# A hybrid encoder block on one core: the attention product in steps of 512 queries, six tiles of P, one tile of diagonals, and low parts of weights on VectorE

## The chip, the core and the metric

The kernel runs on one core of a Trainium2 chip. The core has five engines with an instruction queue each: TensorE (PE in the profile; its weight loads are listed apart as PEld), VectorE (DVE), ScalarE (ACT), GpSimd (POOL) and SyncE (SP), which here issues the DMA transfers. An engine runs its queue in order and waits where an operand or a buffer isn't ready. The metric is the device time of one execution in microseconds, the median of several runs.

## What is computed

One layer of an encoder block over 512 tokens of width 1024: attention heads and state-space heads beside each other, then a gated feed-forward part with a short convolution.

```python
h = rmsnorm(x, norm1_w)
q, k, v, z, xbc, dt_f, dt_b = split(h @ w_in)      # 1024 -> 6176
attn = dilated_attention(partial_rope(q), partial_rope(k), v)     # 16 heads of 64
ssm  = ssm_mixer(z, xbc, dt_f, dt_b, ...)          # 16 heads, 4 groups, chunks of 128, both directions
x = x + concat([attn, ssm]) @ w_out                # 2048 -> 1024
h = rmsnorm(x, norm2_w)
x = x + (silu(gate) * up) @ w_down                 # u = conv(h @ w_up), 1024 -> 2 x 2816 -> 1024
return rmsnorm(x, final_norm_w)
```

The three dilated windows of the attention are computed as one softmax over all 512 keys: each score gets the logarithm of the number of windows in which the pair occurs, or a large negative number where it is in none. All is in float32. Each matrix operand is held as a high and a low part, and a product is the sum of three products (high with high, high with low, low with high), so a matrix product costs three matmuls.

## The kernel before

**Tiles and stages.** Activations lie as 128 partitions by 512 tokens. Weights come by DMA into `raw` tiles; `unit` (L462) splits each into two halves of 128 by 512, a high part `whi` (a copy on ScalarE) and a low part `wlo` (the difference of the two), six buffers each. Which engine makes a difference is read from the table `ENG` (L34), where "A" is ScalarE, "D" VectorE and "P" GpSimd, and a string of several letters is gone through in turn: "lc" and "lx" (the state-space inputs C and X), "lk" (the keys' projections) and "lo" (the output projection) name the low parts that the change touches.

After the first norm comes the woven part. `weave` (L988) takes 50 jobs: eight query and eight key projections (q0 to q7, k0 to k7), three value and three gate projections (the first of each stands ahead of the weave), for each of four groups the inputs B, C and X, the chunk states (s) and the outputs (o) of the state-space part, and eight attention pairs (a0 to a7, two heads each). Each job is a Python generator; its `yield`s divide it into pieces, and `PLAN` (L23) gives each job a due time for its start and its end. At every turn the piece with the earliest due time whose buffers are free goes next. What a `yield` gives back is the piece's share of the job's time; a dictionary names buffers that the next piece needs. This gives a first order of all instructions.

**The order on the engines.** `list_schedule` (L179) then simulates the program with the durations of `cost` (L88), engine by engine, takes the best of some forward and backward passes, and the program is built again with that order fixed on each engine's queue. In the pass (`forward`, L249) an instruction marked as using the port that VectorE and GpSimd share is made longer when the other of the two is busy with such an instruction: by 1 - 0.38 of the other's rest for VectorE, by 1 - 0.8 for GpSimd, with an upper limit (L276 to 280).

**Attention** (`attention_pair`, L926). For each head and each half of the queries (two tiles of 128): two score tiles, each of two matmuls over 512 keys into the bank `s`; VectorE adds the logarithms and takes the minimum (P), ScalarE exponentiates. Then, for two key tiles at a time, four transposes of 128 by 128 into the bank `tr`; ScalarE copies the bank to the high part `PT`, VectorE subtracts it from the bank into the low part `PT`; and four matmuls over 256 queries multiply by the values `V` into the bank `o`. `P` and `PT` have four buffers each, and `tr`, `s` and `o` one bank each.

**Other parts that are named below.** `rope_rows` (L880) ends a projection of q or k: ScalarE copies the bank, VectorE shuffles it (which frees the bank; projections alternate between two banks named `acc`), VectorE multiplies one copy, GpSimd the other, and GpSimd adds them; then follow a high part and a low part, and in `prep_k` (L910) six copies by DMA that spread K over the halves of its tiles. `conv_silu` (L694) evacuates the banks of B, C and X. In `ssm_out` (L796) each of 16 chunks has a tile of decays `D`, two buffers (pool "work", L352): eight diagonals from ScalarE, a scan and two steps on VectorE, and matmuls into the bank `y`. The output projection `out_part` (L1057) starts while the last attention pairs run; the feed-forward part (`up_job`, L1147, and the loop behind it) is one unbroken stream of matmuls.

## Time and profile before

| | |
|---|---|
| median of three runs | 898.53 us (898.29 to 898.71) |
| the profiled execution | 898.54 us |
| its span in the trace | 896.7 us |
| mean granted clock of TensorE | 0.997 of full speed |
| TensorE busy | 881.9 us, 98% |
| VectorE busy | 617.0 us, 69% |
| ScalarE busy | 463.5 us, 52% |
| GpSimd busy | 220.4 us, 25% |
| DMA | 40% of 16 engines, 117 GB/s |

The span runs from the first to the last instruction in the trace; what the execution has beyond it lies around the span. The busy time of an engine is the time in which it has an instruction, waits for a port included. All engine instructions go through one helper, so they all bear line 142, and are told apart by the names of their tiles: `acc<-H,whi` is a matmul into a bank acc with the operands H and whi. A matmul's own duration in a row is longer than the distance to the next, because matmuls are pipelined; the distance between starts is what one costs.

### The profile page before, as it was taken

What the parts mean: (1) busy time and instruction counts of PE and PEld (TensorE: products, weight loads), DVE (VectorE), ACT (ScalarE), POOL (GpSimd) and SP (SyncE); (2) the same over time, 40 slices, a digit from 0 to 9 for tenths busy, and PEclk for the clock granted to TensorE, in tenths of its full rate; (3) what the DMA queues carried; (4) which work ended last, traced back from release to release, by engine and by line L of the source; (5) the groups of instructions that cost most, each with busy time, mean ns of one, the idle gap of its engine ahead of it and who ended that gap; (6) DMA issues with size and microseconds to landing.
All of it is one profiled execution on the core that took longest, in us unless ns stands there. A gap on an engine that the chain in (4) does not pass through costs nothing.

```text
span 896.7 us, 13139 instructions
## 1 busy us (share of the span) xinstructions
PE 881.9 (98%) x4892; PEld 764.9 (85%) x4892; DVE 617.0 (69%) x1038; ACT 463.5 (52%) x963; POOL 220.4 (25%) x187
## 2 busy tenths in 40 slices
PE   7999999999999999999999999999999999999997
PEld 6977888998899889899988998888888888888886
DVE  6766788877896897899843347777777777523323
ACT  6444666556666765767854344444444444323222
POOL 1072564234262543275255300000000000000000
PEclk9999999999999999999999999999999999999999
DMA  8465154534444634235475223333333333222312
GB/s 272 130 146 148 45 124 136 154 85 128 111 113 107 148 111 130 69 92 176 140 240 183 90 77 95 107 103 94 95 94 94 95 111 114 104 95 71 118 48 94
DMA packets 121936, 105.04 MB, mean 117 GB/s; under 512 B 5776, under 2 KB 97808, under 8 KB 121872
## 3 DMA queue, kind: packets, MB, share of 16 engines
q1 hardware_dynamic: 121872, 104.20, 40.1%
q8 instruction: 38, 0.62, 0.3%
q14 instruction: 26, 0.21, 0.1%
HBM read 88.91 MB, written 5.83 MB: 106 GB/s over the span
## 4 chain that ended last, share of the span: by engine, by line
PE 53%; DMA 1%; DVE 0%; ACT 0%; issue 0%; POOLq 0%; POOL 0%; SPq 0%; DVEq 0%; ACTq 0%
PE acc L142 20%; PE tr L142 11%; PE s L142 10%; PE o L142 4%; PE E L142 3%; PE y L142 3%; PE trp L142 2%; DMA mx<-mixA_d 1%; DMA mixA_d<-m 0%; DVE m L142 0%; DVE x L142 0%; ACT fk L142 0%; ACT hl L142 0%; ACT wkp L142 0%; POOLq L1284 0%
## 5 line engine op out<-in xcount | busy, mean ns | idle before, releaser
L142 ACT ACTIVATE whi<-raw 128x512 fp32r<-128x512 f32 x256 | 159.9, 630 | 228.6 <-PE acc L142 142.6
L142 DVE TENSOR_TENSOR wlo<-raw,whi 128x512 fp32r<-128x512 f32 x196 | 140.3, 719 | 135.3 <-ACT whi L142 133.3
L142 PE MATMUL acc<-H,whi 128*128 128x512 f32 x512 | 169.5, 404 | 2.4 <-DVE wkp L142 2.4
L142 POOL TENSOR_TENSOR wlo<-raw,whi 128x512 fp32r<-128x512 f32 x60 | 91.5, 1531 | 131.2 <-ACT whi L142 126.1
L142 PEld LDWEIGHTS acc<-H,whi 128*128 128x128 f32 x512 | 94.1, 190 | 19.9 <-DVE wkp L142 2.8
L142 PE MATMUL acc<-x2w,whi 128*128 128x512 f32 x352 | 109.1, 390 | 0.0
L142 PE MATMUL acc<-H,wlo 128*128 128x512 f32 x256 | 103.1, 403 | 0.0
L142 POOL TENSOR_TENSOR r<-m,half 128x1 f32<-128x1 f32 x4 | 2.2, 548 | 359.2 <-DVE m L142 359.2
L142 PE MATMUL acc<-whi,H 128*128 128x256 f32 x448 | 87.3, 287 | 0.9 <-DVE H L142 0.7
L142 PEld LDWEIGHTS acc<-x2w,whi 128*128 128x128 f32 x352 | 66.0, 188 | 13.7
L142 DVE SCALAR_TENSOR_TENSOR fk<-fk,prm,fk 128x511 f32<-128x511 f32 x88 | 66.1, 751 | 14.2 <-ACT fk L142 12.6
L142 PEld LDWEIGHTS acc<-whi,H 128*128 128x128 f32 x448 | 71.3, 191 | 2.1 <-DVE H L142 1.1
L142 PE MATMUL acc<-x2w,wlo 128*128 128x512 f32 x176 | 68.6, 390 | 0.0
L142 PE MATMUL acc<-wlo,H 128*128 128x256 f32 x224 | 63.6, 284 | 0.0
L142 PEld LDWEIGHTS acc<-H,wlo 128*128 128x128 f32 x256 | 48.6, 190 | 9.1
L142 PE MATMUL o<-PT,V 128*128 128x256 f32 x256 | 54.7, 297 | 0.0
L142 PE MATMUL tr<-x2w,whi 128*128 128x512 f32 x176 | 54.2, 389 | 0.0
L142 PE MATMUL s<-x2w,whi 128*128 128x512 f32 x176 | 54.2, 389 | 0.0
L142 DVE TENSOR_TENSOR PT<-tr,PT 128x512 fp32r<-128x512 f32 x64 | 43.8, 684 | 14.8 <-ACT PT L142 14.4
L142 DVE CUSTOM_DVE_ANT_0 P<-s,lmx 128x512 f32<-128x512 f32 x64 | 43.8, 684 | 13.4 <-PE s L142 11.4
L142 ACT ACTIVATE PT<-tr 128x512 fp32r<-128x512 f32 x64 | 38.1, 595 | 27.4 <-PE tr L142 26.6
L142 ACT ACTIVATE P<-P,mn 128x512 f32<-128x512 f32 x64 | 45.9, 718 | 9.9 <-DVE mn L142 9.5
(267 smaller groups left out, 1960.1 us busy)
## 6 DMA issues: line engine op xcount, KB each, us to landing
raw<-in_w_in_dram SPq DMA_DIRECT2D x48, 512.0 KB, 3.9
raw<-in_w_up_dram SPq DMA_DIRECT2D x44, 512.0 KB, 3.7
raw<-in_w_down_dram SPq DMA_DIRECT2D x22, 512.0 KB, 3.5
A<-step_d SPq DMA_DIRECT2D x16, 512.0 KB, 5.3
raw<-in_w_out_dram SPq DMA_DIRECT2D x16, 512.0 KB, 4.1
K<-K SPq DMA_DIRECT2D x48, 128.0 KB, 2.3
mx<-mixA_d SPq DMA_DIRECT2D x13, 256.0 KB, 3.9
mx<-mixS_d SPq DMA_DIRECT2D x10, 256.0 KB, 3.2
```

The source lines that it names most:

```text
L142: r = fn(*args, **kw)
```

## The change

There are four edits. (1) In `ENG` the low parts "lc", "lx", "lk" and "lo" are all made on VectorE; 60 of them were on GpSimd. (2) In the planner, VectorE and GpSimd exclude each other for the whole rest of the other's instruction, where both use the port; the scan's time per element is taken as 2.09 times the usual instead of twice; and additions of one element count as port users. (3) The diagonals' tile `D` has one buffer instead of two, `P` six instead of four. (4) `attention_pair` makes all four score tiles of a head first and keeps them; then, for each key tile, four transposes fill the bank `tr` with all 512 queries, a high and a low `PT` are made of it, and two matmuls over 512 columns multiply by the values: 128 of them instead of 256 of 256 columns. The pieces' shares become 1.1 for each two score tiles and 1.5 for each two key tiles.

```diff
-    "hb": "A", "lb": "D", "hc": "A", "lc": "P", "hx": "A", "lx": "P", "hz": "A", "lz": "D", "hq": "A",
-    "lq": "D", "hk": "A", "lk": "DPPP", "hv": "A", "lv": "D", "ho": "A", "lo": "PDPP", "hu": "A", "lu": "D",
+    "hb": "A", "lb": "D", "hc": "A", "lc": "D", "hx": "A", "lx": "D", "hz": "A", "lz": "D", "hq": "A",
+    "lq": "D", "hk": "A", "lk": "D", "hv": "A", "lv": "D", "ho": "A", "lo": "D", "hu": "A", "lu": "D",
...
-        return DVE_ONE, False
+        return DVE_ONE, op in ("tensor_add", "tensor_tensor")
...
-        b *= 2
+        b *= 2.09
...
-                other, speed = ("Pool", DVE_SLOWED) if e == "DVE" else ("DVE", POOL_SLOWED)
-                left_to_it = max(0, free.get(other, 0) - t) if shared.get(other) else 0
-                more = min(left_to_it * (1 - speed), hold[i] * (1 / speed - 1))
+                other = "Pool" if e == "DVE" else "DVE"
+                more = max(0, free.get(other, 0) - t) if shared.get(other) else 0
...
-                                  "A": 2, "D": 2, "wk": 2, "wkp": 3, "xs": 2, "P": 4, "PT": 4, "m": 4, "half": 4,
+                                  "A": 2, "D": 1, "wk": 2, "wkp": 3, "xs": 2, "P": 6, "PT": 4, "m": 4, "half": 4,
...
+        den = SM([128, 8], "den", 4)
         for h, me in enumerate((A, B)):
+            P = []
             for hf in range(2):
-                yield {"P": 2, "PT": 4} | ({"m": 1} if h + hf == 0 else {}) | ({"wkp": 1} if hf == 1 else {})
...
+                yield {"P": 2}
                 for q in (2 * hf, 2 * hf + 1):
...
+                    keep(p)
...
+                yield 1.1
+            free(Q[h], Kh[h], Kl[h])
+            for k2 in range(2):
+                yield {"PT": 4} | ({"m": 1} if h + k2 == 0 else {}) | ({"wkp": 1} if k2 == 1 else {})
...
+                for k in (2 * k2, 2 * k2 + 1):
                     b = PS("tr")
-                    for u in range(2):
-                        k = 2 * k2 + u
-                        for q in range(2):
-                            PE.transpose(b[:, u * 256 + q * 128:u * 256 + (q + 1) * 128],
-                                         P[q][:, k * 128:(k + 1) * 128], ident)
+                    for q in range(NQ):
+                        PE.transpose(b[:, q * 128:(q + 1) * 128], P[q][:, k * 128:(k + 1) * 128], ident)
                     ph, pl = T("PT", dt=F32R), T("PT", dt=F32R)
                     cp(ph, b)
                     DVE.tensor_sub(pl, b, f(ph))
-                    for u in range(2):
-                        k = 2 * k2 + u
-                        v = vs[t % 2][k][:, h]
-                        us = slice(u * 256, (u + 1) * 256)
-                        PE.matmul(oh, v, ph[:, us], start=(k == 0), stop=False)
-                        PE.matmul(oh, v, pl[:, us], start=False, stop=(k == NQ - 1))
...
+                    v = vs[t % 2][k][:, h]
+                    PE.matmul(o, v, ph, start=(k == 0), stop=False)
+                    PE.matmul(o, v, pl, start=False, stop=(k == NQ - 1))
...
-                yield 2.6
+                yield 1.5
```

**How the order of the instructions moves, at three places.** The first is the start of the weave, on GpSimd, where the rotary steps of q0 (wkp_120) and k0 (wkp_131) stand. Before:

```order
L142 TENSOR_TENSOR wlo_146_817<-raw_144_814,whi_145_816 128x512
L142 TENSOR_TENSOR wlo_148_821<-raw_144_814,whi_147_820 128x512
L142 TENSOR_TENSOR wkp_120_704<-wkp_120_704,rpt_617 128x512
L142 TENSOR_TENSOR wlo_153_858<-raw_151_855,whi_152_857 128x512
L142 TENSOR_TENSOR wkp_120_704<-wkp_120_704,wkp_121_706 128x512
L142 TENSOR_TENSOR wlo_155_862<-raw_151_855,whi_154_861 128x512
L142 TENSOR_TENSOR wlo_160_899<-raw_158_896,whi_159_898 128x512
L142 TENSOR_TENSOR wkp_131_754<-wkp_131_754,rpt_617 128x512
L142 TENSOR_TENSOR wlo_162_903<-raw_158_896,whi_161_902 128x512
L142 TENSOR_TENSOR wkp_131_754<-wkp_131_754,wkp_132_756 128x512
```

Now GpSimd has there:

```order
L142 TENSOR_TENSOR wkp_120_704<-wkp_120_704,rpt_617 128x512
L142 TENSOR_TENSOR wkp_120_704<-wkp_120_704,wkp_121_706 128x512
L142 TENSOR_TENSOR wkp_131_754<-wkp_131_754,rpt_617 128x512
L142 TENSOR_TENSOR wkp_131_754<-wkp_131_754,wkp_132_756 128x512
L142 TENSOR_TENSOR K_134_762<-wkp_131_754,K_133_761 128x512
```

The low parts between the rotary steps have left GpSimd's queue. On VectorE, at the same place (wkp_121 and wkp_132 are the shuffled copies of q0 and k0, D_265 and its like the decays), before:

```order
L142 SCALAR_TENSOR_TENSOR D_265_1299<-A_264_1298,D_265_1299 128x1024
L142 STREAM_SHUFFLE wkp_121_706<-acc_119_679 128x512
L142 TENSOR_TENSOR D_265_1299<-D_265_1299 128x512
L142 TENSOR_TENSOR wkp_121_706<-wkp_121_706,rpt_617 128x512
L142 SCALAR_TENSOR_TENSOR D_277_1345<-A_276_1344,D_277_1345 128x1024
L142 TENSOR_TENSOR D_277_1345<-D_277_1345 128x512
L142 TENSOR_TENSOR wkp_124_713<-wkp_120_704,Q_122_711 128x512
L142 STREAM_SHUFFLE wkp_132_756<-acc_130_729 128x512
```

Now:

```order
L142 SCALAR_TENSOR_TENSOR D_258_1258<-A_257_1257,D_258_1258 128x1024
L142 SCALAR_TENSOR_TENSOR B_111_656<-acc_110_631,B_111_656 128x512
L142 TENSOR_TENSOR wlo_147_818<-raw_145_815,whi_146_817 128x512
L142 STREAM_SHUFFLE wkp_121_706<-acc_119_679 128x512
L142 TENSOR_TENSOR wlo_149_822<-raw_145_815,whi_148_821 128x512
L142 TENSOR_TENSOR wkp_121_706<-wkp_121_706,rpt_617 128x512
L142 TENSOR_TENSOR D_258_1258<-D_258_1258 128x512
L142 TENSOR_TENSOR wlo_154_859<-raw_152_856,whi_153_858 128x512
L142 TENSOR_TENSOR wkp_124_713<-wkp_120_704,Q_122_711 128x512
L142 TENSOR_TENSOR wlo_156_863<-raw_152_856,whi_155_862 128x512
L142 STREAM_SHUFFLE wkp_132_756<-acc_130_729 128x512
```

The second scan (D_277) has gone from between the two shuffles, and four low parts have come in around them. The second place is TensorE behind the last projection, k7, one round between the transposes of one bank `tr` and the next. Before, a comparable round of the last pairs, between tr_1150 and tr_1153:

```order
L142 MATMUL o_1129_4991<-PT_1143_5027,V_1044_4692 128x256
L142 MATMUL o_1129_4991<-PT_1142_5026,V_1046_4698 128x256
L142 MATMUL o_1129_4991<-PT_1143_5027,V_1046_4698 128x256
L142 MATMUL acc_1198_5220<-whi_1219_5309,hl_1229_5352 128x256
L142 MATMUL s_1170_5118<-K_1099_4887,Q_1025_4552 128x512
L142 MATMUL s_1170_5118<-K_1100_4888,Q_1025_4552 128x512
L142 MATMUL acc_1198_5220<-whi_1219_5309,hl_1228_5351 128x256
L142 MATMUL acc_1198_5220<-wlo_1220_5310,hl_1228_5351 128x256
L142 MATMUL o_1129_4991<-PT_1151_5053,V_1039_4631 128x256
L142 MATMUL acc_1198_5220<-whi_1219_5309,hl_1229_5352 128x256
L142 MATMUL acc_1197_5219<-whi_1219_5309,hl_1231_5369 128x256
L142 MATMUL tr_1153_5061<-ident_86,P_1145_5037 128x128
```

Now, a round from tr_1088 to tr_1091:

```order
L142 MATMUL tr_1088_4746<-ident_86,P_1063_4665 128x128
L142 MATMUL tr_1088_4746<-ident_86,P_1066_4672 128x128
L142 MATMUL tr_1088_4746<-ident_86,P_1069_4679 128x128
L142 MATMUL tr_1088_4746<-ident_86,P_1072_4686 128x128
L142 MATMUL s_1101_4793<-K_952_4196,Q_846_3732 128x512
L142 MATMUL trp_1020_4438<-ident_86,yy_991_4337 128x128
L142 MATMUL trp_1020_4438<-ident_86,yy_960_4237 128x128
L142 MATMUL trp_1020_4438<-ident_86,yy_991_4337 128x128
L142 MATMUL o_1086_4744<-PT_1089_4751,V_1040_4540 128x512
L142 MATMUL tr_1091_4757<-ident_86,P_1063_4665 128x128
L142 MATMUL tr_1091_4757<-ident_86,P_1066_4672 128x128
L142 MATMUL tr_1091_4757<-ident_86,P_1069_4679 128x128
```

The products stand in steps of 512 columns, and fewer matmuls stand between two rounds. The third place is VectorE behind k7, whose K tiles are K_1097 and K_1098 before, K_1082 and K_1083 now (hl are low parts of the output projection's inputs). Before:

```order
L142 TENSOR_TENSOR PT_1084_4820<-tr_1082_4814,PT_1083_4819 128x512
L142 ISA P_1106_4908,mn_1107_4909<-s_1105_4905,lmx_619 128x512
L142 ISA mn_1107_4909 128x1
L142 TENSOR_TENSOR hl_1206_5234<-mx_1204_5231,hl_1205_5233 128x512
L142 CAST K_1097_4885<-wkp_1095_4878 128x512
L142 TENSOR_TENSOR PT_1087_4833<-tr_1085_4827,PT_1086_4832 128x512
L142 TENSOR_TENSOR K_1098_4886<-wkp_1095_4878,K_1097_4885 128x512
L142 ISA P_1115_4941,mn_1116_4942<-s_1114_4938,lmx_619 128x512
```

Now, from the last low part of K on:

```order
L142 TENSOR_TENSOR K_1083_4733<-wkp_1080_4725,K_1082_4732 128x512
L142 ISA P_1108_4810,mn_1109_4811<-s_1107_4807,lmx_619 128x512
L142 ISA mn_1109_4811 128x1
L142 TENSOR_TENSOR hl_1209_5124<-mx_1207_5121,hl_1208_5123 128x512
L142 TENSOR_TENSOR PT_1099_4785<-tr_1097_4779,PT_1098_4784 128x512
L142 ISA P_1111_4817,mn_1112_4818<-s_1110_4814,lmx_619 128x512
L142 ISA mn_1112_4818 128x1
L142 SCALAR_TENSOR_TENSOR D_1186_5044<-A_1185_5043,D_1186_5044 128x1024
L142 TENSOR_TENSOR PT_1116_4828<-tr_1114_4822,PT_1115_4827 128x512
L142 TENSOR_TENSOR D_1186_5044<-D_1186_5044 128x512
```

The last scan (D_1186) now stands ahead of the subtraction PT_1116, behind the last low part of K.

## Rows read from the trace of the kernel before

**Rows 1.** The page, part 1: busy us (share of the span) and instructions by engine.

```profile
PE 881.9 (98%) x4892; PEld 764.9 (85%) x4892; DVE 617.0 (69%) x1038; ACT 463.5 (52%) x963; POOL 220.4 (25%) x187
```

**Rows 2.** Stretches: from:to, us, then PE, PEld, DVE, ACT, POOL busy, PEclk, DMA, GB/s.

```profile
50.00:75.00 25.00, 22.57 (x93) 18.19 (x92) 18.92 (x19) 10.10 (x20) 21.42 (x12) 0.93 0.78 181
575.00:600.00 25.00, 25.00 (x112) 20.71 (x111) 20.22 (x31) 10.11 (x16) 0.00 (x0) 1.00 0.36 106
394.00:424.00 30.00, 29.63 (x204) 26.77 (x204) 29.02 (x58) 22.61 (x55) 16.73 (x15) 1.00 0.49 145
80.00:374.00 294.00, 293.46 (x1802) 260.60 (x1801) 238.03 (x418) 189.01 (x432) 120.67 (x102) 1.00 0.42 112
```

**Rows 3.** TensorE's longest wait: waiting <- waited for: us, times, longest.

```profile
PE acc L142 <- DVE wkp L142: 2.4, 1, 2.4
```

**Rows 4.** Timeline of TensorE: start, us, what [idle before <- releaser].

```profile
452.54 0.52 PE L142 MATMUL o<-PT,V 128*128 128x256 f32 x3
452.90 0.60 PE L142 MATMUL tr<-ident,wkp 128*128 128x128 f32 x4
453.26 0.48 PE L142 MATMUL acc<-whi,hl 128*128 128x256 f32 x2
```

**Rows 5.** The chain that ended last, feed-forward part: start, us, what, count.

```profile
535.40 5.44 PE s L142 x24
```

**Rows 6.** Groups: line, engine, operation, tiles, count | busy us, mean ns | idle before, releasers.

```profile
L142 PE MATMUL o<-PT,V 128*128 128x256 f32 x256 | 54.7, 297 | 0.0
L142 DVE TENSOR_TENSOR wlo<-raw,whi 128x512 fp32r<-128x512 f32 x196 | 140.3, 719 | 135.3 <-ACT whi L142 133.3 <-ACT m L142 1.4 <-PE acc L142 0.2
L142 POOL TENSOR_TENSOR wlo<-raw,whi 128x512 fp32r<-128x512 f32 x60 | 91.5, 1531 | 131.2 <-ACT whi L142 126.1 <-PE acc L142 2.5 <-issue 2.4
L142 PE MATMUL acc<-H,whi 128*128 128x512 f32 x512 | 169.5, 404 | 2.4 <-DVE wkp L142 2.4
L142 PE MATMUL acc<-x2w,whi 128*128 128x512 f32 x352 | 109.1, 390 | 0.0
L142 ACT ACTIVATE D<-ident,dt 128x128 f32<-128x128 f32 x128 | 42.5, 391 | 8.4 <-DVE dt L142 4.2 <-PE y L142 4.1
```

**Rows 7.** Timeline from 51 to 69 us: VectorE, GpSimd and TensorE.

```profile
51.12 1.29 POOL L142 TENSOR_TENSOR wlo<-raw,whi 128x512 fp32r<-128x512 f32 x1 [2.73 <-ACT whi L142]
...
53.43 2.28 DVE L142 TENSOR_TENSOR_SCAN D<-A,D 128x1024 f32<-128x1024 f32 x1
...
56.11 0.75 DVE L142 STREAM_SHUFFLE wkp<-acc 128x512 f32<-128x512 f32 x1
...
59.04 3.38 DVE L142 TENSOR_TENSOR_SCAN D<-A,D 128x1024 f32<-128x1024 f32 x1
...
60.23 3.27 POOL L142 TENSOR_TENSOR wlo<-raw,whi 128x512 fp32r<-128x512 f32 x1
...
63.46 1.74 POOL L142 TENSOR_TENSOR wkp<-wkp,wkp 128x512 f32<-128x512 f32 x1
...
67.66 0.73 DVE L142 STREAM_SHUFFLE wkp<-acc 128x512 f32<-128x512 f32 x1
68.45 1.02 PE L142 MATMUL acc<-H,whi 128*128 128x512 f32 x2 [2.42 <-DVE wkp L142]
```

**Rows 8.** Timeline of one round of the attention product, before k7's last matmul.

```profile
409.17 0.60 PE L142 MATMUL tr<-ident,P 128*128 128x128 f32 x4
...
409.87 0.60 ACT L142 ACTIVATE PT<-tr 128x512 fp32r<-128x512 f32 x1 [1.35 <-PE tr L142]
...
410.50 0.69 DVE L142 TENSOR_TENSOR PT<-tr,PT 128x512 fp32r<-128x512 f32 x1 [0.23 <-ACT PT L142]
```

**Rows 9.** Timeline of k7: its last matmul, the last copy of K, the first scores.

```profile
410.54 0.40 PE L142 MATMUL acc<-H,wlo 128*128 128x512 f32 x1
...
422.09 0.46 SPq L142 DMA_DIRECT2D K<-K  x1
...
424.22 0.39 PE L142 MATMUL s<-K,Q 128*128 128x512 f32 x1
```

More of the change, by code (lines that the diff above doesn't have):

```diff
@@ L84 @@
 PE_NS, PE_LEAST, PE_F32 = (13.3, 0.4167), 109, 480
-DVE_SLOWED, POOL_SLOWED = 0.38, 0.8
 def cost(name, args, kw):
@@ L927, in attention_pair @@
         Kh, Kl = KK
+        den = SM([128, 8], "den", 4)
         for h, me in enumerate((A, B)):
+            P = []
             for hf in range(2):
-                yield {"P": 2, "PT": 4} | ({"m": 1} if h + hf == 0 else {}) | ({"wkp": 1} if hf == 1 else {})
-                if hf == 0:
-                    o = PS("o")
-                    if h == 0:
-                        m = T("m")
-                        keep(m)
-                        den = SM([128, 8], "den", 4)
-                P = []
+                yield {"P": 2}
                 for q in (2 * hf, 2 * hf + 1):
@@ L947, in attention_pair @@
                     P.append(p)
-                oh = o[:, hf * 256:(hf + 1) * 256]
-                for k2 in range(2):
-                    b = PS("tr")
-                    for u in range(2):
-                        k = 2 * k2 + u
-                        for q in range(2):
-                            PE.transpose(b[:, u * 256 + q * 128:u * 256 + (q + 1) * 128],
-                                         P[q][:, k * 128:(k + 1) * 128], ident)
+                yield 1.1
+            free(Q[h], Kh[h], Kl[h])
+            for k2 in range(2):
+                yield {"PT": 4} | ({"m": 1} if h + k2 == 0 else {}) | ({"wkp": 1} if k2 == 1 else {})
+                if k2 == 0:
+                    o = PS("o")
+                    if h == 0:
+                        m = T("m")
+                        keep(m)
+                for k in (2 * k2, 2 * k2 + 1):
+                    b = PS("tr")
+                    for q in range(NQ):
+                        PE.transpose(b[:, q * 128:(q + 1) * 128], P[q][:, k * 128:(k + 1) * 128], ident)
                     ph, pl = T("PT", dt=F32R), T("PT", dt=F32R)
@@ L958, in attention_pair @@
                     DVE.tensor_sub(pl, b, f(ph))
-                    for u in range(2):
-                        k = 2 * k2 + u
-                        v = vs[t % 2][k][:, h]
-                        us = slice(u * 256, (u + 1) * 256)
-                        PE.matmul(oh, v, ph[:, us], start=(k == 0), stop=False)
-                        PE.matmul(oh, v, pl[:, us], start=False, stop=(k == NQ - 1))
-                if hf == 1:
+                    v = vs[t % 2][k][:, h]
+                    PE.matmul(o, v, ph, start=(k == 0), stop=False)
+                    PE.matmul(o, v, pl, start=False, stop=(k == NQ - 1))
+                if k2 == 1:
                     tm = T("wkp")
@@ L969, in attention_pair @@
                     DVE.tensor_add(m[me], tm[me], o[me])
-                    free(Q[h], Kh[h], Kl[h])
+                    free(*P)
                     if h == 1:
                         free(*vs[t % 2])
-                yield 2.6
+                yield 1.5
         yield {"wkp": 1}
```

## The prediction

> **What bounds the kernel now.** The totals by engine come first: TensorE is busy 881.9 of 896.7 us, VectorE 617.0, GpSimd 220.4 [rows 1]. The busy time by stretch comes next, to see whether TensorE is also at its best pace. From 575 to 600 us, in the feed-forward part, it does 112 matmuls with nothing in between; from 80 to 374 us, in the woven part (projections, attention and state-space work mixed by a plan), it is busy 293.46 of 294.00; from 394 to 424, where the last attention pairs run, 29.63 of 30.00, and there VectorE has 29.02 of 30 [rows 2]. So TensorE sets the time nearly everywhere, and the time is the sum of its steps and of its few waits. One stretch is worse: from 50 to 75 us it has 22.57 of 25 and a mean granted clock of 0.93 [rows 2]. Its waits, read third, hold one long one: 2.4 us, for a VectorE result of the rotary step [rows 3]. An edit pays here only if it shortens TensorE's steps or takes away that wait, and it costs if it opens a new wait.
>
> The profiled execution took 898.54 us, 1.84 more than its span; the median of the runs is 898.53. I sum against 898.54.
>
> **The product with the values, in steps of 512.** 256 matmuls over 256 columns become 128 over 512 [rows 6]; the columns are the same. Three steps of 256 columns take 0.36 us from the first start (452.54) to the next instruction (452.90), 0.120 us each [rows 4]; 24 steps of 512 take 5.44 us, 0.227 each [rows 5]. So 256 x 0.120 = 30.7 us become 128 x 0.227 = 29.0: **-1.7 us**, all on TensorE's path. By the Trainium skill, "TensorE: Matmul & The Clock Gate", section on the back-to-back issue gap, the fixed part of a step is about 2.5 ns, by which this term would be 128 x 2.5 ns = 0.3 us and the sum 1.4 higher; the rows have 13 ns, and they decide.
>
> **Low parts of weights to VectorE.** 60 subtractions leave GpSimd, where they last 1531 ns in the mean, for VectorE, where the other 196 last 719 [rows 6]: VectorE gets some 60 x 0.69 = 41 us more. In the mean it has room (238.03 of 294 from 80 to 374); in the stretch from 394 to 424 it has almost none [rows 2]. On TensorE's path the move costs nothing where the halves lie three jobs ahead in their six buffers; where VectorE is full it delays what stands behind in its queue, and that is priced with the last pairs below.
>
> **The wait at 68 us.** Here the move helps. GpSimd does a low part from 60.23 for 3.27 us, beside a VectorE scan of 3.38 us (59.04), and only then, at 63.46, the rotary sum of q0; ScalarE, VectorE and the shuffle that frees the bank of k0 follow (shuffle at 67.66), and TensorE, out of matmuls at 66.0, goes on at 68.45 [rows 7]. In the new order GpSimd has no low part before these two sums, and VectorE only one scan instead of two before the shuffle of k0 (front part, first excerpt). The step then reads: shuffle of q0 at about 56.1 as now, 0.75 long, then a low part and the multiply, 0.69 each (the row at 410.50), GpSimd's sum 1.29 to about 59.5, ScalarE 0.60, VectorE's low half and one more low part, 0.69 each, and the shuffle of k0 done at about 62.3 [rows 7, 8], where the bank is wanted at 66.0. The wait of 2.4 us goes, and with it the slow clock behind it: 7% of 25 us, 1.7 us [rows 2, 3]. **-4.1 us.** What is late next: the bank of c0, whose chain of evacuations is covered by one projection's 24 matmuls, 5.4 us [rows 5], and needs about 4.5, an estimate of six steps of 0.69 to 0.75.
>
> **The planner's new rules, and one buffer of diagonals.** They cost no work; they move the order. One buffer makes ScalarE's eight diagonals wait for the matmuls of the chunk before: 8 x 0.39 and the scan of 2.28 and two VectorE steps of 0.69, some 7 us [rows 6 to 8] for each of 16 chunks that lie over 300 us, hidden behind the weave. It bites at one place, where a scan now stands in VectorE's queue just ahead of a subtraction that TensorE waits for (next).
>
> **The last attention pairs.** Each key tile is now four transposes into one bank, ScalarE's copy, VectorE's subtraction, and only then the next four. Rows for that round: transposes at 409.17, copy at 409.87 for 0.60, subtraction at 410.50 for 0.69, bank free at 411.2 [rows 8]: **2.0 us**, for which TensorE needs other work. In the middle of the weave the new order has it. Behind k7, the last projection, it hasn't: between the transposes tr_1088 and tr_1091 stand (second excerpt) one score matmul, three transposes and one product, 0.23 + 0.27 + 0.23, and the four transposes themselves 0.36 (452.90 to 453.26 in [rows 4]): 1.1 us, short by 0.9. Counted in the same way the next two rounds are short by 0.25 and 0.15; tr_1114 to tr_1117 by 1.2 (between its fourth transpose and the next bank stand 0.5 us); the two after it by 0.3 and 0.65; and in the last head the fourth transpose comes alone and the product behind it at once, short of a copy by 0.9. Together 4.4 us. The old order's comparable round (same excerpt) has nine matmuls of 256 columns and two of 512 beside its transposes, 1.5 us and 1.9 in all, and the trace has no wait there.
>
> That is with VectorE free at each step. It isn't: it stands at 29 of 30 us [rows 2], and ahead of these subtractions the new queue holds scores' reductions, a low part of the output weights, a cast that waits for GpSimd, and at PT_1116 the scan (third excerpt). One step of 0.69 ahead in each of six rounds makes 4.4 into 8.5; the scan once, 2.28, makes it 9 to 10. Also k7 itself: from its last matmul (410.54) over the rotary steps and the last copy of K (422.09) to the first scores (424.22) it takes 13.7 us [rows 9], and the new order has some 9.2 us of matmuls there (its steps counted at the durations above) besides waits, so the waits for K and for the bank lie in part on each other. I take **+7.5 us**, nearer to the upper end, since the row of VectorE there is full; ends 4.4 and 10.
>
> **Elsewhere in the weave.** The row from 80 to 374 has 0.54 us of idle TensorE [rows 2]. The new order has a few rounds short by 0.2 to 0.5 (a state sum, the first transposes of the residual). **+0.8**, between 0 and 2.
>
> Sum: 898.5 - 1.7 - 4.1 + 7.5 + 0.8 = **901.0 us**.
>
> **Rivals.** *Only the bare rounds wait.* If VectorE's subtraction starts right behind each copy, the last pairs cost 4.4 and the rest 0.4: 898.54 - 1.7 - 4.1 + 4.4 + 0.4 = 897.5, which can't be told from before. For it: the planner put these instructions where it expected them ready. Against it: 29.02 of 30.
>
> *The weave gets faster: the freed port.* The projections' matmuls last 404 ns in the woven part and 390 in the feed-forward part [rows 6], 14 ns on the 512 of this group, 7 us, of which the slow clock is a part: small delays that no list of waits shows. VectorE and GpSimd hold each other up: the scan of 3.38 and the low part of 3.27 at 60 us [rows 7] against 2.28 and 1.29 alone. If half of the 7 us goes with GpSimd's 60 instructions, and the last pairs cost the bare 4.4, the time is 898.5 - 5.8 + 4.4 - 3.6 = 893.5. It decides where VectorE's queue, not TensorE's own pace, sets those 14 ns; against it stands that VectorE takes on 41 us. The Trainium skill, "SBUF — State Buffer", section on the two separate sides, says that the two engines' common port is an exclusive lock for a whole instruction; by that rule the two rows at 60 us are one engine waiting out the other, and the trace agrees (3.27 is 1.29 and about 2).
>
> *VectorE becomes the bound.* If the 41 us make its queue fall behind in the middle too, from the point where its share passes the 97% that it has between 394 and 424, banks come free late as at 68 us. Two such places at 4.1 us each: 901 + 8 = 909, or 905 for one. For it: 238 us and two thirds of 41 in 294 are 90%. Against it: the mean still leaves 10%.
>
> *The wait at 68 us stays* (the queue of VectorE, with two more low parts ahead of the shuffle, takes the part of GpSimd's): 905.
>
> **How the numbers follow.** Chances: the forecast 0.50 (its own range 898.5 to 904), bare rounds 0.24, freed port 0.17, VectorE bound or the old wait kept 0.09. A measurement of this kernel can tell about 0.2%, 1.8 us. The forecast's case lies above 900.3 in 0.41 and within in 0.09; bare rounds are within in 0.18 and faster in 0.06; freed port is faster; the last slower. So faster 0.23, same 0.27, slower 0.50. The range of 893.5 to 905.5 leaves out the lower half of the freed port and most of the last case.
>
> **What would show it.** The clock from 50 to 75 us at 1.00 and no TensorE wait over 1 us there: the 4.1. The PT,V group at 128 instructions of 512 columns: the 1.7. New TensorE waits of 0.5 to 2 us, ended by VectorE's PT, ScalarE's PT or the copies of K, between 380 and 425 us: the 7.5. Wrong it would be if TensorE's list of waits behind the last projection sums to less than 4 or more than 10, or if one over 1 us turns up between 80 and 370.

## The result: slower by 0.7%, and where the profile shows it

| | before | changed kernel |
|---|---|---|
| median of three runs | 898.53 us | 904.89 us (904.14 to 905.66) |
| ratio to before, 95% interval | 1 | 1.0073 (1.0058 to 1.0087) |
| the profiled execution | 898.54 us | 905.66 us |
| its span | 896.7 us | 903.9 us |

The changed kernel is slower, by 6.4 us in the medians and by 7.2 us in the two profiled spans, which are compared in what follows. The forecast was 901.0 in a range of 893.5 to 905.5.

The first part of the page of the changed kernel, busy time by engine, answers to [rows 1]:

```profile
PE 888.8 (98%) x4764; PEld 760.6 (84%) x4764; DVE 637.4 (71%) x1098; ACT 464.1 (51%) x963; POOL 125.9 (14%) x127
```

TensorE has 128 instructions fewer and is busy longer. GpSimd gave up 94.5 us, VectorE took on only 20.4, though its 60 new subtractions last 43 us: the rest it got back on its other instructions. The stretches answer to [rows 2], with two more at the end (from:to, us, then PE, PEld, DVE, ACT and POOL busy, PEclk, DMA share, GB/s):

```profile
50.00:75.00 25.00, 24.93 (x111) 20.29 (x110) 21.03 (x27) 10.53 (x18) 7.08 (x5) 1.00 0.75 180
80.00:374.00 294.00, 292.98 (x1705) 254.44 (x1704) 246.12 (x440) 188.13 (x434) 83.07 (x80) 1.00 0.42 112
394.00:424.00 30.00, 28.34 (x167) 23.16 (x166) 27.51 (x56) 25.84 (x66) 7.00 (x6) 0.99 0.38 110
375.00:475.00 100.00, 95.42 (x593) 82.06 (x591) 79.33 (x153) 67.86 (x161) 24.84 (x23) 0.97 0.48 145
423.20:430.00 6.80, 6.80 (x25) 5.88 (x26) 5.33 (x14) 3.50 (x10) 0.80 (x2) 0.50 0.21 69
```

The first row is the gain: TensorE full and at its full clock where it had 22.57 of 25 and 0.93. The fourth row is the loss: 4.58 us of idle TensorE, where the kernel before has 0.51 in the same 100 us. The last row is a loss that idle time doesn't show: TensorE is busy all the time, at half its clock.

**Lost time by stretch.** Since matmuls overlap, a sum of idle times is too low. A better measure comes from the starts of all matmuls in a trace: from the distance between a start and the next one is taken what an undisturbed step needs (0.227 us for 512 columns and 0.120 for 256 [rows 4, 5]; 0.109 is taken for 128 or fewer); the rest is lost time. From before to the changed kernel it goes from 7.24 to 7.59 us in the first 50 us, from 5.24 to 1.77 between 50 and 100, from 10.54 to 12.08 between 100 and 375, and from 3.99 to 14.59 between 375 and 475. That is 0.35 - 3.47 + 1.54 + 10.60; with the 1.7 us of steps saved, and 0.3 saved behind the last matmul, it makes 7.0 of the 7.2 us. The steps are put into this account, so that it closes says nothing of their size. All these times are of one traced execution of each kernel.

The 10.60 behind 375 us lie in these places: 0.84 from 375 to 395, ahead of the last pairs' rounds; 2.87 from 395 to 423.2, in the rounds behind k7; 3.21 from 423.2 to 430.0, where the granted clock is 0.50; 0.06 from there to 450; 1.94 from 450 to 460, in the last head; and 1.68 from 460 to 475, where the last pair's result is awaited.

**The gain at 68 us.** The timeline of VectorE and GpSimd in the changed kernel (start, us, engine, instruction, idle before it and its releaser), to set against [rows 7]:

```profile
56.46 0.75 DVE L142 STREAM_SHUFFLE wkp<-acc 128x512 f32<-128x512 f32 x1
56.50 1.29 POOL L142 TENSOR_TENSOR wkp<-wkp,rpt 128x512 f32<-128x512 f32 x1 [35.70 <-ACT wkp L142]
...
59.09 1.60 POOL L142 TENSOR_TENSOR wkp<-wkp,wkp 128x512 f32<-128x512 f32 x1 [1.29 <-DVE wkp L142]
59.47 1.77 DVE L142 TENSOR_TENSOR wlo<-raw,whi 128x512 fp32r<-128x512 f32 x1
...
62.81 0.75 DVE L142 STREAM_SHUFFLE wkp<-acc 128x512 f32<-128x512 f32 x1
```

GpSimd waits for its rotary step instead of being late to it, the sum of q0 is done at 60.69 instead of 65.20, and the shuffle of k0 starts at 62.81 instead of 67.66, ahead of the 66 us at which TensorE wants the bank. The prediction had it done at 62.3; it is done at 63.56. The difference is in the fourth line: a low part that takes 1.77 us on VectorE beside a GpSimd sum that ends at 60.69. The two still hold each other up, on the rotary steps that stay on GpSimd. The Trainium skill, "SBUF — State Buffer", section on the two separate sides, calls the common port an exclusive lock; 0.69 us behind 60.69 would be 61.38, and the row ends at 61.24, so the trace agrees to 0.14 us.

**The loss behind k7.** The six longest of the eleven entries in the list of TensorE's waits between 375 and 475 us in the changed kernel (waiting <- waited for: us, times, longest):

```profile
PE o L142 <- ACT PT L142: 0.8, 1, 0.8
PE tr L142 <- DVE PT L142: 0.5, 2, 0.3
PE y L142 <- DVE D L142: 0.4, 1, 0.4
PE trp L142 <- POOL yy L142: 0.4, 1, 0.4
PE acc L142 <- POOL hl L142: 0.4, 1, 0.4
PE acc L142 <- DVE x L142: 0.4, 1, 0.4
```

No wait is long, and the list sums to 4.1 us, 3.5 of them behind k7's last matmul at 408.45. The kernel before has two of 0.2 us in this stretch. The timeline of one round, and of eight short matmuls ahead of it and behind it:

```profile
407.33 1.00 PE L142 MATMUL y<-X,D 128*128 128x64 f32 x8
...
418.46 2.29 DVE L142 TENSOR_TENSOR_SCAN D<-A,D 128x1024 f32<-128x1024 f32 x1
...
419.44 0.33 PE L142 MATMUL tr<-ident,P 128*128 128x128 f32 x1
419.81 0.59 ACT L142 ACTIVATE PT<-tr 128x512 fp32r<-128x512 f32 x1
...
420.66 0.67 DVE L142 TENSOR_TENSOR PT<-tr,PT 128x512 fp32r<-128x512 f32 x1
...
421.38 0.66 PE L142 MATMUL tr<-ident,P 128*128 128x128 f32 x4 [0.29 <-DVE PT L142]
...
423.14 1.95 PE L142 MATMUL y<-X,D 128*128 128x64 f32 x8 [0.42 <-DVE D L142]
```

From the fourth transpose (419.44) over copy and subtraction to the next transposes (421.38) are 1.94 us. The prediction's round of 2.0 counts from the first transpose [rows 8]; from the fourth, some 0.33 us later, it would be 1.7, so this one is some 0.25 longer. The scan does stand ahead of the subtraction, as the order showed, and holds it from about 420.4 to 420.66 only, since the round itself came late. Behind several such pauses the clock falls: the same eight matmuls last 1.00 us at 407 and 1.95 at 423. At a granted clock of 0.50, which is 1.2 of 2.4 GHz, the 6.8 us from 423.2 to 430.0 hold 3.4 us of work. So of the 10.60 us that the changed kernel loses more behind 375, **3.4 are the clock** and 7.2 are waits and their neighbourhood. This is so in the traced execution, at a mean granted clock of 0.993; the two others have 0.994 and 0.995, and where theirs fell isn't on record.

The last of these waits are at the end of the chain. The timeline of the changed kernel where the result of the last pair is stored, loaded again, split and multiplied:

```profile
462.70 0.32 SPq L142 DMA_DIRECT2D mixA_d<-m  x1
...
464.77 0.33 SPq L142 DMA_DIRECT2D mx<-mixA_d  x1
...
470.78 0.63 ACT L142 ACTIVATE hl<-mx 128x512 fp32r<-128x512 f32 x1 [1.46 <-DMA mx<-mixA_d]
471.46 0.39 PE L142 MATMUL acc<-whi,hl 128*128 128x256 f32 x1 [0.32 <-ACT hl L142]
```

The store stands at 455.23 in the kernel before, 7.5 us earlier, and TensorE doesn't wait for it there.

### The profile page after: what moved, and what is told of

It reads as the page before. It is cut to its first block, busy times and chain, and to the rows that moved or that the text cites. A ratio compares the mean times of both kernels' runs of the same rounds, so it can differ in the third digit from the quotient of the medians.

```text
span 903.9 us, 12826 instructions
## 1 busy us (share of the span) xinstructions
PE 888.8 (98%) x4764; PEld 760.6 (84%) x4764; DVE 637.4 (71%) x1098; ACT 464.1 (51%) x963; POOL 125.9 (14%) x127
## 4 chain that ended last, share of the span: by engine, by line
PE 93%; DVE 3%; ACT 1%; DMA 1%; issue 1%; SPq 0%; POOLq 0%; POOL 0%; ACTq 0%
PE acc L142 49%; PE tr L142 13%; PE s L142 13%; PE o L142 6%; PE y L142 5%; PE E L142 4%; PE trp L142 4%; DMA x<-in_x_dram 1%; DMA raw<-in_w_in_dram 1%; DVE D L142 1%; DVE B L142 0%; ACT whi L142 0%; SPq L142 0%; DVE wlo L142 0%; DVE PT L142 0%
## 5 line engine op out<-in xcount | busy, mean ns | idle before, releaser
L142 DVE TENSOR_TENSOR wlo<-raw,whi 128x512 fp32r<-128x512 f32 x256 | 184.6, 725 | 151.2 <-ACT whi L142 149.4
L142 PE MATMUL acc<-whi,H 128*128 128x256 f32 x448 | 89.3, 288 | 0.4 <-DVE H L142 0.2
L142 PE MATMUL o<-PT,V 128*128 128x512 f32 x128 | 55.5, 443 | 1.0 <-ACT PT L142 0.8
L142 ACT ACTIVATE D<-ident,dt 128x128 f32<-128x128 f32 x128 | 42.3, 391 | 18.3 <-PE y L142 14.1
```

The source lines that it names most:

```text
L142: r = fn(*args, **kw)
```

## The experiments

The theory after the result (A): TensorE waits for the rounds of the last pairs, since one bank takes all four transposes of a key tile; the gain at 68 us is GpSimd's free queue. Rivals: (B) VectorE's 41 us more are the loss; (C) the planner's order is. The table gives each run's median, its ratio to runs of the kernel before on the same chip with the 95% interval, the time of the one execution that was traced, the lost time of three stretches of it worked out as above, how much of the last stretch's is the low clock (half of the time at 0.50), and when the last pair's last product starts. The first 50 us, where weights and parameters are awaited, vary from 6.7 to 9.0 us between traces and are left out. Where a text below gives a difference between two runs in us, it is of the medians; the runs were on several chips, and by the ratios such a difference can come out up to 0.8 us otherwise. The plan is made anew for every edit, so each run also has an order of instructions of its own.

| run | us | ratio | traced | 50-100 | 100-375 | 375-475 | of it clock | last product |
|---|---|---|---|---|---|---|---|---|
| before | 898.53 | 1 | 898.54 | 5.24 | 10.54 | 3.99 | 0 | 452.8 |
| changed kernel | 904.89 | 1.0073 (1.0058-1.0087) | 905.66 | 1.77 | 12.08 | 14.59 | 3.4 | 459.6 |
| e1 low parts alone | 899.61 | 1.0012 (1.0001-1.0022) | 898.80 | 2.27 | 12.60 | 4.98 | 0 | 451.1 |
| e2 attention and pools alone | 901.07 | 1.0024 (1.0013-1.0036) | 899.25 | 3.12 | 11.08 | 8.48 | 0 | 453.3 |
| e3 planner alone | 899.54 | 1.0009 (0.9996-1.0022) | 898.28 | 3.38 | 9.98 | 6.42 | 0 | 452.5 |
| e4 second bank, pairs 6 and 7 | 897.64 | 0.9994 (0.9983-1.0004) | 897.82 | 1.77 | 12.04 | 6.09 | 0 | 447.5 |
| e5 old pairs 6 and 7 | 902.35 | 1.0041 (1.0026-1.0056) | 900.24 | 1.80 | 12.51 | 8.81 | 0 | 453.6 |
| e6 low parts back | 906.90 | 1.0087 (1.0067-1.0107) | 907.51 | 3.22 | 13.22 | 11.80 | 0 | 461.9 |
| e7 output's low parts back | 904.60 | 1.0066 (1.0050-1.0081) | 904.60 | 1.74 | 12.41 | 12.19 | 0 | 459.0 |
| e8 planner back | 900.06 | 1.0011 (1.0001-1.0021) | 900.16 | 1.50 | 10.12 | 10.04 | 0 | 455.7 |
| e9 second bank, planner back | 895.32 | 0.9971 (0.9959-0.9982) | 895.11 | 1.53 | 10.37 | 6.13 | 0 | 443.5 |
| e10 two D, four P | 906.17 | 1.0081 (1.0065-1.0098) | 905.26 | 1.51 | 10.35 | 14.84 | 1.7 | 461.1 |
| e11 one planner number | 903.46 | 1.0050 (1.0033-1.0067) | 903.46 | 1.73 | 11.50 | 12.32 | 1.7 | 459.1 |
| e12 second bank, all pairs | 899.05 | 1.0009 (1.0000-1.0018) | 900.16 | 2.24 | 10.95 | 8.15 | 0 | 451.1 |

### One part alone: e1, e2, e3

e1 is the kernel before with

```diff
-    "hb": "A", "lb": "D", "hc": "A", "lc": "P", "hx": "A", "lx": "P", ... "lk": "DPPP", ... "lo": "PDPP",
+    "hb": "A", "lb": "D", "hc": "A", "lc": "D", "hx": "A", "lx": "D", ... "lk": "D", ... "lo": "D",
```

> The kernel before with one edit, all low parts of weights on VectorE; attention, pools and planner as before. Theory A (the loss comes from the new attention rounds behind k7, the gain from GpSimd's free queue at 68 us): the wait of 2.4 us at 68 us and its slow clock go, nothing new behind k7, 894 to 896 us. Theory B (VectorE's 41 us more are the loss): new TensorE waits ended by VectorE between 380 and 450 us, 902 us or more.

The gain is there, 3.0 us between 50 and 100, and behind 375 only 1.0 is lost, so B by itself isn't the main loss. Yet the kernel isn't faster: 2.1 us are lost between 100 and 375. The largest piece, in the windows and in the timeline of e1:

```profile
137.00:140.00 3.00, 1.54 (x11) 1.12 (x10) 2.56 (x7) 1.12 (x4) 0.41 (x1) 1.00 0.38 74
140.00:143.00 3.00, 3.00 (x17) 2.51 (x17) 3.00 (x6) 2.68 (x8) 2.41 (x2) 0.67 0.00 0
```

```profile
133.95 1.17 DVE L142 TENSOR_TENSOR wlo<-raw,whi 128x512 fp32r<-128x512 f32 x1
135.04 1.78 DVE L142 TENSOR_TENSOR D<-D 128x512 f32<-128x512 f32 x1
...
138.41 0.67 DVE L142 TENSOR_TENSOR D<-D,CM 128x512 f32<-128x512 f32 x1
...
139.22 0.96 PE L142 MATMUL y<-X,D 128*128 128x64 f32 x7 [1.46 <-DVE D L142]
```

A low part of 1.17 us now stands ahead of the decays that TensorE waits for, 1.46 us, and the step of the decays behind it takes 1.78. The clock is at 0.67 in the 3 us behind: it is granted at 0.51 from 141.0 to 144.4, which costs 1.7. This is the prediction's third rival on a small scale, one place at some 3 us, of which the rest of the stretch gives one back.

e2 is the kernel before with the new `attention_pair` and the line of the pools (D 1, P 6):

> The kernel before with the new attention pairs and its pools (one D, six P), low parts on GpSimd and the planner as before. Theory A: the wait at 68 us stays, the product gives 1.7 back, behind k7 some 11 us are lost: 906 to 909 us. Theory B: with VectorE relieved of the 41 us the rounds behind k7 wait less than half of that, 897 to 902 us.

The time lies in what theory B expected, and so do the 4.5 us more behind 375, less than half of 11. So the new attention alone doesn't make the loss; whether the low parts make the rest is tested from the other side by e6. The traced execution is the fastest of ten, 1.8 us below their median. The wait that e2 keeps near 71 us is 2.0 us, for C, not for the rotary step.

e3 is the kernel before with the hunks of `cost` and `forward` alone:

> The kernel before with the planner's new rules alone (its costs and the exclusion on the port). Theory A: the order moves, no work does; within 2 us of 898.5, and the wait at 68 us mostly stays, since GpSimd still has its low parts there. Rival C (the rules remove the wait at 68 us by themselves): 894 to 895 us.

Within the interval of no change, as expected; but behind 375 the new order loses 2.4 us more, balanced by 1.9 won between 50 and 100, where the wait stays (2.2 us) and the clock doesn't fall behind it.

Added up, the three parts alone lose 0.99 + 4.49 + 2.43 = 7.9 us behind 375 over the kernel before. The changed kernel loses 10.60 there, of which the clock is 3.4; the 7.2 that are left are near the sum of the parts, each read from one trace.

### Take away the one bank: e4, e9, e12

e4 is the changed kernel with

```diff
-                    b = PS("tr")
+                    b = PS("trp" if t >= 6 and k % 2 else "tr")
```

> The changed kernel, but in the last two attention pairs every second key tile transposes into the bank trp instead of tr, so that a round need not wait for the subtraction of the one before. Theory A (the one bank makes TensorE wait): the waits between 408 and 430 us go from some 3 us to under 1, the granted clock there stays at 1.00, 896 to 900 us. Theory B (VectorE's queue): VectorE is as full, the waits only move to the products, 903 to 906 us.

7.3 us come back (904.89 to 897.64), by an edit that takes nothing off VectorE. The windows of e4:

```profile
375.00:475.00 100.00, 97.82 (x633) 86.05 (x632) 83.04 (x161) 70.44 (x170) 24.64 (x22) 1.00 0.53 162
408.00:430.00 22.00, 20.05 (x128) 16.16 (x126) 20.97 (x45) 19.20 (x48) 3.87 (x3) 1.00 0.39 108
```

The expectation was right in the time and the clock, and wrong on how: between 408 and 430 TensorE is idle for 1.95 us here, no less than the 1.66 of the changed kernel in the same stretch. TensorE's waits in e4 from 375 to 475 us are two:

```profile
PE s L142 <- DVE mn L142: 1.3, 3, 0.5
PE tr L142 <- DVE PT L142: 0.4, 1, 0.4
```

From 395 to 423.2 us, e4 loses 4.07 us where the changed kernel loses 4.62: with the second bank TensorE waits there for VectorE's reductions of the scores, and VectorE is theory B's cause. So the runs don't show that the bank makes the loss in this stretch; e3, with the old attention, loses 4.45 in it. What goes is the rest: the slow clock, and the late end of the last pair. Its last product stands at 447.5 instead of 459.6, and with it the result of the pair, which the output projection needs: the waits in the last head at 450 and those between 470 and 475 us (for hl from ScalarE and GpSimd, and for x) are gone: 4.14 us of lost time from 450 to 475 become 0.15. So the single bank costs most as a *chain*, as these times are read here: eight rounds of the last pair, one behind the other, end later than the work that covers them.

e9 has the second bank and the old `cost` and `forward`:

> The changed kernel with the two edits together that each took most of its loss back: the old planner rules, and the second bank for every other key tile of the last two pairs. If the bank and the order are separate parts of the loss behind 375 us, both go, and what is left is the gain at 68 us and the longer steps: 893 to 896 us. If the second bank takes the place of the order: 897 to 899 us.

895.32 us, faster than both kernels: 0.29% below the kernel before. The time is that of the first expectation, its reason isn't. Behind 375 us e9 loses 6.13 us and e4, with the new rules, 6.09: there the second bank takes the place of the order. What the old rules add lies elsewhere: 1.67 us less from 100 to 375, and 1.2 less in the first 50, where the clock in e4's trace is low from 12.0 to 15.4. TensorE's waits from 375 to 475 us in e9:

```profile
PE trp L142 <- ACT yy L142: 1.2, 1, 1.2
PE tr L142 <- DVE PT L142: 0.5, 1, 0.5
PE acc L142 <- ACT hl L142: 0.4, 1, 0.4
PE o L142 <- ACT PT L142: 0.3, 1, 0.3
```

and one round with the two banks:

```profile
409.01 0.60 PE L142 MATMUL trp<-ident,P 128*128 128x128 f32 x4
409.11 0.69 DVE L142 TENSOR_TENSOR PT<-tr,PT 128x512 fp32r<-128x512 f32 x1
...
409.93 0.60 PE L142 MATMUL tr<-ident,P 128*128 128x128 f32 x4
410.28 1.43 PE L142 MATMUL o<-PT,V 128*128 128x512 f32 x4
```

Two sets of transposes start 0.92 us apart, where a round through one bank takes some 2 us, and four products stand together.

e12 uses the second bank in all eight pairs (`"trp" if k % 2 else "tr"`), with the old planner:

> The run with the old planner rules and the second bank, with that bank in all eight pairs instead of the last two. If the rounds in the middle of the weave are covered by other work, as the prediction took them, there is nothing to win: within 1 us of 895.3. If they cost small waits there: 893 us or less. If the bank trp is then missing for the transposes of the state-space outputs: 897 us or more.

The time is that of the third case, 899.05, 3.7 us above e9, but its reason isn't there: the list of TensorE's waits has none for the bank trp. Two lines of it:

```profile
PE s L142 <- DVE mn L142: 2.7, 4, 1.0
...
PE y L142 <- DVE D L142: 1.0, 1, 1.0
```

TensorE waits for VectorE's reductions of the scores and for decays, once each near 98 and 378 us for about 1 us. So nothing is won in the middle (10.95 us lost from 100 to 375, 10.37 in e9), as the prediction's reading of the covered rounds would have it; why VectorE comes late in this order wasn't followed further.

### Undo one part of the change: e5 to e8, e10, e11

e5 keeps the old `attention_pair` for the last two pairs:

```diff
-        add("a", t, attention_pair, [f"q{t}", f"k{t}", f"v{t // 2}"], 10.9)
+        add("a", t, attention_pair_old if t >= 6 else attention_pair, [f"q{t}", f"k{t}", f"v{t // 2}"], 10.9)
```

> The changed kernel, but with the old attention pair (half the queries at a time, steps of 256) for the last two pairs; the other six keep the steps of 512. Theory A (the new rounds of the last pairs are the loss, with VectorE's full queue): behind k7 about as in the run with the low parts alone, 896 to 899 us, clock 1.00 from 400 to 450 us. Theory B (VectorE's queue alone): 902 us or more.

2.5 us come back, not 6 to 9, and the result lies on B's side of the expectation. Lost time behind 375 falls from 14.59 to 8.81, with the clock at 1.00. This is near the 7.4 that the kernel before, the low parts alone and the planner alone add up to (3.99 + 0.99 + 2.43): the new rounds of the last pairs are their own part, and the other two parts stay. The traced execution is the fastest of eight, 2.1 us below their median, so the trace doesn't show all that the median holds.

e6 is the changed kernel with the old `ENG`:

> The changed kernel with one edit undone: the low parts go back to GpSimd; new attention, pools and planner stay. If the new rounds and the low parts of the same stretch make the loss together: 900 to 902 us, no fall of the clock behind 420 us, last product of the last pair some 5 us earlier than the changed kernel's 459.6. If the low parts have nothing to do with it: 904 us or more, since the wait at 68 us comes back.

906.90: both halves of the first expectation fail. The wait near 70 us is back (1.9 us), and behind 375 still 11.8 us are lost, at a clock of 1.00, and 0.96 more from 475 to 490; the last product is the latest of all. The low parts on VectorE aren't what makes the last pairs late.

e7 gives back those of the output weights only (`"lo": "PDPP"`):

> The changed kernel, with only the low parts of the output projection's weights back on GpSimd three times in four; those of C, X and K stay on VectorE. If these are what stands in VectorE's queue ahead of the last pairs' subtractions: the start keeps its gain, the end is as in the run with the new attention alone, 897 to 900 us. If not: 903 to 906 us.

904.60, no change against the changed kernel. A longer wait turned up in its place, in the timeline of e7:

```profile
416.49 0.60 ACT L142 ACTIVATE PT<-tr 128x512 fp32r<-128x512 f32 x1 [0.47 <-PE tr L142]
...
416.81 2.28 DVE L142 TENSOR_TENSOR_SCAN D<-A,D 128x1024 f32<-128x1024 f32 x1
...
419.02 0.66 DVE L142 TENSOR_TENSOR PT<-tr,PT 128x512 fp32r<-128x512 f32 x1
...
419.73 0.66 PE L142 MATMUL tr<-ident,P 128*128 128x128 f32 x4 [1.82 <-DVE PT L142]
```

Here the scan costs what the prediction feared: it starts while ScalarE's copy is still under way, the subtraction waits from 417.1 to 419.0, and TensorE for 1.82 us.

e8 is the changed kernel with the old `cost` and `forward`:

> The changed kernel with the old planner rules. If the order that the new rules give is part of the loss: 901 us or less. If the rules are neutral, as alone on the kernel before: 904 to 906 us.

900.06, 4.8 us back, where the rules alone (e3) cost nothing. Of the lost time, 1.96 us less lie between 100 and 375 and 4.55 behind 375. But the clock is at 1.00 from 100 to 475 us in e8, and the changed kernel without its 3.4 us of slow clock would have 11.2 there against 10.04. So rival C has 1.2 us in the waits behind 375 and 2.0 ahead of it, and for the rest, 3.4, it is whether the clock falls. VectorE is as full as before (81.15 us of the 100, 79.33 in the changed kernel).

e10 has two tiles of D and four of P (`"D": 2`, `"P": 4`):

> The changed kernel with two tiles of diagonals and four of P, as before. If the single tile D puts the scan ahead of a subtraction that TensorE waits for (the prediction's term, up to 2.3 us, and the fall of the clock behind it): 899 to 902 us. If it is the attention's single bank alone, or if four tiles of P hold back the next scores: 904 to 907 us.

906.17, as in the second case. P changed together with D, so the time alone doesn't clear the single tile of diagonals. The trace says more: with two of them the scan isn't ahead of the subtraction, and TensorE waits all the same, in the timeline of e10:

```profile
417.27 0.33 PE L142 MATMUL tr<-ident,P 128*128 128x128 f32 x1
417.36 0.59 ACT L142 ACTIVATE wkp<-o 64x512 f32<-64x512 f32 x1
417.98 0.60 ACT L142 ACTIVATE PT<-tr 128x512 fp32r<-128x512 f32 x1
...
418.67 0.68 DVE L142 TENSOR_TENSOR PT<-tr,PT 128x512 fp32r<-128x512 f32 x1
...
419.40 0.66 PE L142 MATMUL tr<-ident,P 128*128 128x128 f32 x4 [1.80 <-DVE PT L142]
```

The subtraction starts 0.09 us behind the copy's end. The round takes 2.13 us from the fourth transpose to the next, without a scan; what makes it longer is on ScalarE, which copies the bank `o` first and comes to this bank 0.38 us behind the transpose's end. Here the clock falls too, to 0.50 from 421.0 to 424.4 us.

e11 undoes one number (`b *= 2.09` to `b *= 2`):

> The changed kernel with one number of the planner undone, the scan's time per element 2 instead of 2.09 times the usual. It costs no work and says nothing of the port. If the late loss is made by the rules' meaning: 904 to 906 us. If it hangs on the order that the plan happens to fall into: 2 us or more to either side, with other places of waiting between 400 and 475 us.

903.46, between the two expectations: 1.4 us less than the changed kernel, with intervals that overlap, and 2.3 us less lost behind 375, with one wait of 1.85 us that the changed kernel doesn't have. Of these 2.3 us, some 1.7 are the clock, which is at 0.50 from 418.0 to 421.4 us here and for twice as long in the changed kernel. So a number that costs no work moves the waits to other places, and their sum by some 0.6 us. How much of e8's 4.8 us is the rules' meaning, and how much the order into which the plan happens to fall, these runs don't tell; it stays open.

## Why the prediction was right, and which terms were off

- **The sign and the range** held: 904.89 against 901.0, in 893.5 to 905.5, near the upper end. In part this is luck: a loss that the sum doesn't have, the clock's 3.4 us, and one that it has and the runs don't show, VectorE's queue, lie on either side.
- **Steps of 512, -1.7**: not shown. From the start of one product to the next matmul the median is 0.119 us for 256 columns before and 0.237 for 512 in the changed kernel (0.233 to 0.235 in the other kernels that have these steps in all pairs), so that 30.5 us become 30.3, or 29.8 at best. The 0.227 of the unbroken stream isn't reached among the other matmuls.
- **The wait at 68 us, -4.1**: measured -3.5 between 50 and 100 us: the clock's 1.7 as forecast, and 1.8 for the wait. In the ten kernels with the low parts of C, X and K on VectorE 1.5 to 2.3 us are left there; with them on GpSimd (e2, e3, e6) it is 3.1 to 3.4, with a wait of 1.9 to 2.2 us.
- **The last pairs, +7.5, between 4.4 and 10**: the mis-sized term, +10.6 measured. Without the clock 7.2 are left, but that this is near 7.5 is luck: the rounds behind k7 and in the last head lose 4.8 us more than before, near the 4.4 of the bare rounds, and the 3.1 that the prediction put on top for VectorE's queue aren't in them. By the prediction's own signs the term is wrong: 10.6 is beyond its upper end, TensorE's list of waits behind the last projection sums to 3.5 us, less than 4, and no wait for a PT or for K between 380 and 425 us reaches 0.5. Two things are missing in the term. One is the clock, 3.4 us: the prediction priced the slow clock behind the wait at 68 us and forgot that waits of its own could bring it back. The other, 1.7 us, is the late result of the last pair, which the output projection waits for between 470 and 475 us; the prediction counted rounds and not where their chain ends.
- **Why they wait** was right in the first half: one bank, since a second one takes 8.5 us off, the 3.4 of the clock and 4.0 behind 450 us among them (e4). In the rounds ahead of 423.2 us it takes only 0.6 off, and what makes TensorE wait there stays open. The second half, VectorE's queue made longer by the moved low parts, is a small part: alone they lose 1.0 us there (e1), and with the low parts on GpSimd the changed kernel is no better (e6, e7), though e4's waits for the scores' reductions show that VectorE's queue counts once the bank doesn't. VectorE's busy share there didn't rise: 23.73 us of the 25 from 400 to 425, where the kernel before has 24.05, with waits of TensorE of 0.2 us at most. The scan ahead of a subtraction is real (1.82 us in e7), but without it a round waits as long (e10).
- **The planner's rules** got no term of their own. Alone they cost nothing (e3); together with the other edits 4.8 us (e8), most of it by the clock, and some 2 us from 100 to 375, where e9 against e4 has 1.7 as well.
- **Elsewhere, +0.8**: +1.5 between 100 and 375, no wait over 0.5 us, but see e1. Some 0.8 of it lies right behind the products: 2.5 us are lost behind the 78 there, 1.7 behind the 168 of the kernel before.
- **The rivals.** Bare rounds (897.5) had 4.4 us for the last pairs; for the rounds themselves, 4.8, this was nearer than the forecast's 7.5, but it has neither the clock nor the late result. The freed port (893.5): the projections' matmuls went from 404 to 401 ns, which on 512 of them is 1.5 us, the slow clock at 68 us included; the low parts on VectorE alone brought no freer weave (12.60 us lost between 100 and 375 in e1, 10.54 before). VectorE as the bound at one place, and the old wait kept, both gave 905, and that the time is 904.89 speaks for neither: the longest wait between 80 and 370 us is 0.5 us, and from 50 to 75 the clock is 1.00.

## What to carry to other kernels

Where a larger step needs a whole bank, count the round through that bank (write, copy, subtract, write again) at the place where the least other work is left, and follow its chain to whoever needs the last result; a second bank there alone was worth 7.3 us, which brought the time back to that of the kernel before; with the old planner rules too it became a gain of 0.29%. And where new short waits are forecast one after the other, put a price on the clock as well: here it was a third of what was lost behind 375 us.

## What the runs showed of the hardware that was not expected

The clock of TensorE doesn't follow the idle time in a simple way. In the changed kernel it fell to 0.50 behind pauses of which none was longer than 0.5 us by the list of waits, TensorE having been busy 8.76 of the 10 us ahead of the fall at 423.2; in e1 it fell to 0.51 behind 8.54 busy of 10, with one wait of 1.46 us. In e7 TensorE was busy only 6.04 of the 10 us from 410 to 420, with a wait of 1.82 us, and the granted clock stayed at 1.00, there and in the 10 us behind; in e6 with 7.01 of the 10 us from 420 to 430 as well. The low clock, once granted, lasted 6.8 us although TensorE was busy without a gap. What decides between these cases the runs don't show. It also differs between executions of one kernel: those of the kernel before that were taken beside e1 have mean granted clocks from 0.992 to 0.999, at 896.45 to 900.86 us.
